# Forgetting attention: value products of an even and an odd head as one piece of TensorE's work, alternating block by block

## The chip, the cores and the metric

The kernel runs on one core of a Trainium2 chip. The metric is the device time of one execution in microseconds. Before the change three runs took 1273.55, 1274.48 and 1274.74 us; the median is 1274.48 us.

## What is computed

Two decoder layers on 512 tokens, with 16 learned meta tokens ahead of them (528 rows, 1024 features, fp32). Each layer projects its rows into the inputs of three mixers (retention, pooling, forgetting attention), puts their outputs side by side, projects them back, adds the residual and normalises; then a gated feed-forward layer does the same. The change is in the forgetting attention, which has six heads of 64 features:

```python
c = jnp.cumsum(logf.astype(jnp.float32), axis=1).transpose(0, 2, 1)
qf = q.astype(jnp.float32) * (d ** -0.5)
...
s = jnp.einsum('bihd,bjhd->bhij', qb, kf)
s = s + cb[..., :, None] - c[..., None, :]
mask = (kpos[None, :] <= qpos[:, None]) & key_ok[None, :]
s = jnp.where(mask, s, NEG_INF)
p = jax.nn.softmax(s, axis=-1)
return jnp.einsum('bhij,bjhd->bihd', p, vf)
```

The last line is the one whose order of work changes.

## The kernel before

**Staging.** The tokens are cut into five chunks: 16 meta tokens (chunk 0), then four of 128 (chunks 1 to 4). Large products (input weights, output weights, feed-forward) run with every operand split in a high and a low part, three products each: lines 195, 196 and 197 (`mm3`). Weights come from memory as chunks of 128 x 1024, are split by ScalarE (line 174) and by VectorE or GpSimd (line 138), and are kept in four buffers.

**What sets the order.** TensorE's program order is made by `Plan`: each run of its work is a `Piece` with an assumed cost, dependencies with assumed delays (the table `LAG`), a priority, and a count of the buffers that it holds. `Plan.run` walks a clock of assumed times and takes, of the pieces that should be ready and whose buffers fit, the first by priority. Pieces of attention have priority 5, the products of the input weights 9, so the latter fill the time between. The times are assumptions that decide the order alone; on the chip TensorE executes that order and waits where an input isn't there. The other engines' instructions are put in order by the framework.

**Forgetting attention**, per chunk c = 1 to 4 and head h = 0 to 5, over the key blocks of 128 tokens up to the chunk's own (c blocks):
- `fox_q` (lines 621 to 630) splits two heads' queries; GpSimd makes the low part (`qb`).
- `fox_score` (667 to 684): two products for the scores (lines 634 and 635; for chunk 4 four, into the one buffer `s2`), then masked with a maximum on VectorE (679), Exp with a sum on ScalarE (680), and scaled by the reciprocal of the sum on VectorE (682) and, for the meta tokens, on GpSimd (683).
- `fox_turn` (686 to 693): one transpose per block on TensorE (691) into PSUM, and a copy into a buffer `pt` (693), by VectorE for even heads and by ScalarE for odd ones.
- `fox_value` (695 to 703): one product per block, accumulated in PSUM tile `o`. The output has 64 partitions: the lower 64 for even heads, the upper 64 for odd ones; heads 0 and 1 share columns 0 to 127, 2 and 3 the next 128, 4 and 5 the next.
- `fox_meta` (705 to 716): the transposed weights of the meta tokens (708), and their products onto `o` (714), after which the chunk goes to the mix.

A value product is plain fp32 and leaves two records in the trace. Its stationary operand has 128 rows and 64 columns. Scores and `pt` share seven buffers `tmp` by tag, and `holds` counts them; `one` are four PSUM buffers. Pooling's sums (`pool_sums`, lines 816 to 834) run on VectorE in the same stage, and `pool_mix` (841) at its end. After it come the output weights' products over `mixAf` and `mixBf`.

## Time and profile before

| | us |
|---|---|
| median of three runs | 1274.48 |
| span of the profiled execution | 1271.5 |
| TensorE busy | 1234.6 |
| VectorE busy | 646.6 |
| ScalarE busy | 479.9 |
| GpSimd busy | 337.7 |
| value products (line 701), 240 records, busy | 30.3 |
| transposes (line 691), 120 records, busy | 21.1 |

The page gives the profiled execution's span, from its first to its last instruction; its time from outside is not given apart from the three runs, whose median is 3.0 us above that span. Records of TensorE overlap: a product's record lasts from its start to its modelled end, while the next starts already. How long a run of products holds up the engine is read from the starts in the timeline of the trace: from one group's start to the next group's start. A row of the timeline has start, duration, engine, line, operation, tiles, stationary shape, moving shape and the count of records put together (x8).

### The profile page before, as it was taken

The numbers are of one execution on the slowest core, as the hardware profiler recorded it, in microseconds if no ns is written. First come the engines' busy times: TensorE is split into PE (matmuls) and PEld (weight loads), VectorE is DVE, ScalarE is ACT, GpSimd is POOL, SyncE is SP. The second block draws the span as 40 slices with busy tenths as digits, with TensorE's granted clock in tenths as the row PEclk, the third lists the DMA queues.
The fourth block names the chain that finished last, engine by engine and source line by source line (L and its number), as shares of the span: only waits on it lengthen the run. The fifth ranks groups of instructions, "written<-read, shape, count | busy, mean of one in ns | idle before, by whom it ended". The sixth has DMA issues, their size and how long they took to land. (4 is left out here: it accounts for less than half of the span.)

```text
span 1271.5 us, 21413 instructions
## 1 busy us (share of the span) xinstructions
PE 1234.6 (97%) x8650; PEld 1145.8 (90%) x8650; DVE 646.6 (51%) x1257; ACT 479.9 (38%) x893; POOL 337.7 (27%) x375
## 2 busy tenths in 40 slices
PE   7999999889999999999999999998999999999997
PEld 6999989889999999999999899997888888888886
DVE  7575677963333333333384756789632333332226
ACT  5436544543232232222264366455423232221112
POOL 5423339740001100010055243498600000000004
PEclk9999999999999999999999999999899999999999
DMA  6431212423222223233343221134222232222222
GB/s 231 125 99 51 68 34 101 135 98 100 96 88 86 98 84 96 77 90 92 108 143 123 80 80 59 34 118 153 94 84 99 85 99 95 88 100 100 99 91 75
DMA packets 41506, 122.58 MB, mean 96 GB/s; under 512 B 6392, under 2 KB 12696, under 8 KB 41408
## 3 DMA queue, kind: packets, MB, share of 16 engines
q1 hardware_dynamic: 41408, 121.22, 29.1%
q8 instruction: 68, 1.11, 0.4%
q14 instruction: 30, 0.25, 0.1%
HBM read 115.22 MB, written 2.10 MB: 92 GB/s over the span
## 5 line engine op out<-in xcount | busy, mean ns | idle before, releaser
L195 PE MATMUL acc<-xh,w 128*128 128x256 f32 (+2 forms) x1920 | 589.7, 307 | 0.4 <-DVE ka L138 0.4
L196 PE MATMUL acc<-xl,w 128*128 128x256 f32 (+2 forms) x1920 | 582.0, 303 | 1.5 <-POOL xl L138 1.0
L197 PE MATMUL acc<-xh,w 128*128 128x256 f32 (+2 forms) x1920 | 581.8, 303 | 0.0
L138 DVE TENSOR_TENSOR w<-raw,w 128x1024 fp32r<-128x1024 f32 (+1 forms) x181 | 217.4, 1203 | 332.7 <-ACT w L174 332.4
L195 PEld LDWEIGHTS acc<-xh,w 128*128 128x128 f32 x1920 | 363.4, 189 | 18.1 <-issue 1.6
L196 PEld LDWEIGHTS acc<-xl,w 128*128 128x128 f32 x1920 | 364.1, 190 | 16.4 <-POOL xl L138 1.9
L197 PEld LDWEIGHTS acc<-xh,w 128*128 128x128 f32 x1920 | 363.1, 189 | 13.7
L174 ACT CAST w<-raw 128x1024 fp32r<-128x1024 f32 (+1 forms) x211 | 218.8, 1038 | 301.7 <-PE acc L197 121.1
L138 POOL TENSOR_TENSOR w<-raw,w 128x256 fp32r<-128x256 f32 (+1 forms) x74 | 120.6, 1635 | 69.7 <-ACT w L174 61.7
L361 POOL TENSOR_TENSOR y<-xh,xl 128x256 f32<-128x256 f32 (+1 forms) x64 | 51.2, 827 | 225.2 <-DVE g8Bl L138 93.8
L256 POOL TENSOR_TENSOR r<-r,mhalf 128x1 f32<-128x1 f32 (+3 forms) x18 | 14.7, 819 | 324.6 <-DVE r L255 324.6
L138 POOL TENSOR_TENSOR xl<-y,xh 128x256 fp32r<-128x256 f32 (+1 forms) x57 | 49.6, 886 | 22.3 <-ACT xh L271 16.3
L981 ACT ACTIVATE y<-acc 128x272 f32<-128x272 f32 (+1 forms) x44 | 17.2, 392 | 89.0 <-PE acc L197 89.0
L981 ACT ACTIVATE sa<-acc 128x512 f32<-128x512 f32 (+1 forms) x24 | 13.5, 563 | 88.4 <-PE acc L197 88.4
L984 DVE TENSOR_TENSOR sa<-sa,acc 128x512 f32<-128x512 f32 (+1 forms) x24 | 15.4, 642 | 59.0 <-PE acc L197 57.9
L285 DVE SCALAR_TENSOR_TENSOR y<-y,acc 128x256 f32<-128x256 f32 (+1 forms) x48 | 20.1, 420 | 44.5 <-PE acc L197 44.3
L984 DVE TENSOR_TENSOR y<-y,acc 128x272 f32<-128x272 f32 (+1 forms) x44 | 18.9, 429 | 40.4 <-PE acc L197 40.4
L290 POOL TENSOR_TENSOR y<-y 128x256 f32<-128x256 f32 (+1 forms) x12 | 11.0, 914 | 106.3 <-DVE y L285 106.3
L294 ACT ACTIVATE y<-y 128x256 f32<-128x256 f32 (+1 forms) x42 | 17.6, 419 | 54.6 <-DVE y L285 54.5
L680 ACT ACTIVATE p<-p,sm 128x144 f32<-128x144 f32 (+3 forms) x48 | 27.6, 574 | 17.7 <-DVE sm L679 16.1
L683 POOL TENSOR_SCALAR pm<-p,sm 128x16 f32<-128x16 f32 x48 | 21.8, 455 | 43.8 <-DVE sm L681 42.5
L290 DVE TENSOR_TENSOR y<-y 128x256 f32<-128x256 f32 (+1 forms) x30 | 32.1, 1071 | 2.5 <-POOL y L290 1.2
(1000 smaller groups left out, 1916.9 us busy)
## 6 DMA issues: line engine op xcount, KB each, us to landing
raw<-in_w SPq DMA_DIRECT2D x88, 512.0 KB, 3.3
raw<-in_w_in SPq DMA_DIRECT2D x42, 512.0 KB, 4.0
raw<-in_w_out SPq DMA_DIRECT2D x32, 512.0 KB, 3.4
raw<-in_w2b SPq DMA_DIRECT2D x22, 512.0 KB, 3.3
raw<-in_w2a SPq DMA_DIRECT2D x18, 512.0 KB, 3.4
raw<-in_w2a SPq DMA_DIRECT2D x9, 384.0 KB, 3.2
xin<-in_x SPq DMA_DIRECT2D x4, 512.0 KB
out<-y SPq DMA_DIRECT2D x12, 128.0 KB, 1.8
```

Of the source, the lines that this page charges most:

```text
L138: return eng.tensor_tensor(lo, full, hi.bitcast(F32), op=ALU.subtract)
L174: nc.scalar.copy(w[:, 0, :n], raw[:, :n])
L195: nc.tensor.matmul(ps, lhsT=wh, rhs=hi, start=first, stop=False)
L196: nc.tensor.matmul(ps, lhsT=wh, rhs=lo, start=False, stop=False)
L197: nc.tensor.matmul(ps, lhsT=wl, rhs=hi, start=False, stop=last)
L285: nc.vector.scalar_tensor_tensor(y, y, ALPHA, ps, op0=ALU.mult, op1=ALU.add)
L290: (nc.gpsimd if CFG[f"s{i}"] else nc.vector).tensor_tensor(self.s, self.seen[0] if i == 1 else self.s, y, op=ALU.add)
L361: nc.gpsimd.tensor_tensor(y, hi[:, o:].bitcast(F32), lo[:, o:].bitcast(F32), op=ALU.add)
L680: nc.scalar.activation(out=p[:, :NM + nk], in_=p[:, :ce], func=AF.Exp, scale=-1.0, bias=sm[:, 0:1], accum_out=sm[:, 1:2])
L683: nc.gpsimd.tensor_scalar(F[c, "pm"][:, h, :], p[:, :NM], sm[:, 2:3], 1.0, op0=ALU.mult, op1=ALU.mult)
L981: nc.scalar.activation(out=s, in_=ps, func=AF.Silu)
L984: nc.vector.tensor_tensor(s, s, ps, op=ALU.mult)
```

## The change

The values of heads 2i and 2i + 1 become one piece. Its loop goes over the key blocks, and in each block does the even head's product and then the odd head's. The piece waits for both heads' transposes and holds both `pt` buffers. Its assumed cost is 0.26 us per block for two heads, where it was 0.16 per block and head. Products, operands and sums are the same, and so are all other pieces. Below line 712 the lines of the changed kernel move down by 3, in the plan by 3 to 7: 701 becomes 704, 708 becomes 711, 714 becomes 717, 841 becomes 844. The other lines of the diff drop comments and docstrings.

```diff
-        def fox_value(c, h):
+        def fox_value(c, i):
+
             nk = CH[c][1] - NM
-            if h == 0:
+            if i == 0:
                 F[c, "o"] = one()
-            o, pt = F[c, "o"], F.pop((c, "pt", h))
+            o, pts = F[c, "o"], [F.pop((c, "pt", 2 * i + j)) for j in range(2)]
             for b in range(nk // P):
-                nc.tensor.matmul(o[64 * (h % 2):64 * (h % 2) + 64, (h // 2) * P:(h // 2 + 1) * P],
-                                 lhsT=vt["vf"][:, b, h * 64:(h + 1) * 64], rhs=pt[:, b * P:(b + 1) * P],
-                                 start=(h < 2 and b == 0), stop=False, skip_group_check=True)
+                for j, pt in enumerate(pts):
+                    h = 2 * i + j
+                    nc.tensor.matmul(o[64 * j:64 * j + 64, i * P:(i + 1) * P],
+                                     lhsT=vt["vf"][:, b, h * 64:(h + 1) * 64], rhs=pt[:, b * P:(b + 1) * P],
+                                     start=(i == 0 and b == 0), stop=False, skip_group_check=True)
...
                 tn = add(lambda c=c, h=h: fox_turn(c, h), 0.11 * (nk // P), [(sc_, lag("p") + nk / 450.0)], 5)
-                prev_v = add(lambda c=c, h=h: fox_value(c, h), 0.16 * (nk // P),
-                             [(tn, lag("pt")), prev_v] + [(vf[b], lag("vt")) for b in range(1, c + 1)], 5)
                 sc_.holds("tmp", 2, tn)
+                if h % 2 == 0:
+                    even = tn
+                    continue
+                prev_v = add(lambda c=c, h=h: fox_value(c, h // 2), 0.26 * (nk // P),
+                             [(even, lag("pt")), (tn, lag("pt")), prev_v] + [(vf[b], lag("vt")) for b in range(1, c + 1)], 5)
+                even.holds("tmp", 1, prev_v)
                 tn.holds("tmp", 1, prev_v)
-                if h == 0:
+                if h == 1:
                     first_v = prev_v
```

Since costs and dependencies of the pieces change, the plan puts other work differently too. Three places on TensorE show it.

In layer 0, chunk 3, the order before has these rows, the values of two heads (L701) with the scores of a later head between them:

```order
L197 MATMUL acc<-xh,w 128x256
L701 MATMUL one<-pt,vtf 64x128 x3
L634 MATMUL one<-ka,qa 128x400
L635 MATMUL one<-kb_1115,qb_136 128x400
L701 MATMUL one<-pt,vtf 64x128 x3
L691 MATMUL one<-c_ident,p 128x128 x3
```

In the changed kernel the same chunk has:

```order
L197 MATMUL acc<-xh,w 128x272
L704 MATMUL one<-pt,vtf 64x128 x6
L691 MATMUL one<-c_ident,p 128x128 x3
L634 MATMUL one<-ka,qa 128x400
L635 MATMUL one<-kb_1115,qb_136 128x400
```

Two runs of three products have become one of six. Over the whole kernel the order has 33 runs of value products before and 20 now.

At the start of chunk 4 in layer 0 stand, before, the values and transposes of a head of chunk 3 and then the first scores of chunk 4 (tile `s`):

```order
L701 MATMUL one<-pt,vtf 64x128 x3
L691 MATMUL one<-c_ident,p 128x128 x3
L634 MATMUL s_2299<-ka,qa 128x272
L635 MATMUL s_2299<-kb_133,qb_137 128x272
L634 MATMUL s_2299<-ka,qa 128x256
L635 MATMUL s_2299<-kb_133,qb_137 128x256
L195 MATMUL acc<-xh,w 128x272
```

and now a pair of chunk 3, the first scores of chunk 4, and the transposes of the last two heads of chunk 3 with those of the meta tokens (L711):

```order
L704 MATMUL one<-pt,vtf 64x128 x6
L634 MATMUL s_2301<-ka,qa 128x272
L635 MATMUL s_2301<-kb_133,qb_137 128x272
L634 MATMUL s_2301<-ka,qa 128x256
L635 MATMUL s_2301<-kb_133,qb_137 128x256
L691 MATMUL one<-c_ident,p 128x128 x6
L711 MATMUL one<-c_ident,pm 96x128
```

The scores of chunk 4 have moved ahead of two heads' transposes.

At the end of layer 1's mixing the order before has the last products of the input weights, pooling (L841) and the first output weights; values and meta products (L701, L714) stand 39 and 24 products earlier:

```order
L195 MATMUL acc<-xh,w 128x256
L196 MATMUL acc<-xl,w 128x256
L197 MATMUL acc<-xh,w 128x256
L841 MATMUL one<-pu_7523,pw 128x256
L841 MATMUL one<-pu_7524,pw 128x256
L841 MATMUL one<-pu_7523,pw 128x256
L841 MATMUL one<-pu_7524,pw 128x256
L195 MATMUL acc<-mixAf,w 128x256
```

The changed kernel has there:

```order
L197 MATMUL acc<-xh,w 128x256
L844 MATMUL one<-pu_7523,pw 128x256
L844 MATMUL one<-pu_7524,pw 128x256
L704 MATMUL one<-pt,vtf 64x128 x8
L844 MATMUL one<-pu_7523,pw 128x256
L844 MATMUL one<-pu_7524,pw 128x256
L717 MATMUL one<-pmt,vbd 128x128 x3
L195 MATMUL acc<-mixAf,w 128x256
```

The last pair and the meta products now come after the last input weights.

## The prediction

> **What bounds the kernel now.** I read the page first, then the busy time by stage, the waits of TensorE in the two stages that the change touches, and last the order of time around single runs of value products, where the prices are.

> ```profile
> span 1271.5 us, 21413 instructions
> PE 1234.6 (97%) x8650; PEld 1145.8 (90%) x8650; DVE 646.6 (51%) x1257; ACT 479.9 (38%) x893; POOL 337.7 (27%) x375
> ...
> core 0: us, PE busy (x) PEld busy (x) DVE busy (x) ACT busy (x) POOL busy (x), PEclk, DMA share, GB/s
> 130.00:160.00 30.00, 29.39 (x242) 27.25 (x242) 20.97 (x63) 16.61 (x45) 11.98 (x18) 1.00 0.17 55
> 160.00:200.00 40.00, 39.47 (x305) 35.27 (x304) 30.06 (x68) 17.48 (x40) 21.11 (x26) 1.00 0.13 41
> 770.00:800.00 30.00, 30.00 (x238) 26.84 (x236) 23.24 (x69) 19.17 (x51) 11.73 (x20) 1.00 0.11 37
> 800.00:835.00 35.00, 35.00 (x280) 32.64 (x280) 23.32 (x50) 14.45 (x32) 22.04 (x26) 1.00 0.14 46
> ```

> TensorE (PE) is busy 1234.6 of 1271.5 us. The forgetting attention of layer 0 lies at about 115 to 200 us and that of layer 1 at about 740 to 830. In the four windows PE is busy 133.9 of 135 us, at a granted clock of 1.00; the next engine, VectorE (DVE), is busy 97.6. In these stages PE has hardly a hole, so time taken from its row comes off the end, unless a hole opens. The holes that are there:

> ```profile
> PE one L708 <- ACT pt L693: 0.6, 1, 0.6
> PE one L691 <- DVE p L682: 0.5, 1, 0.5
> ...
> PE acc L196 <- DVE xl L845: 0.4, 1, 0.4
> ```

> Two waits of 1.1 us together in layer 0 (135 to 201 us), one of 0.4 us in layer 1 (768 to 843 us).

> **The value products as they are.** A busy PE is not a PE at its peak, so I read starts, not durations. One fp32 product leaves two records.

> ```profile
> L701 PE MATMUL one<-pt,vtf x240: 272/273/324, 139.7 to 827.0; 128*64 128x128 f32 x120
> ...
> 181.69 0.29 PE L196 MATMUL acc<-xl,w 128*128 128x272 f32 x1
> 181.82 0.28 PE L197 MATMUL acc<-xh,w 128*128 128x272 f32 x1
> 182.04 1.09 PE L701 MATMUL one<-pt,vtf 128*64 128x128 f32 x8
> 183.06 0.44 PE L691 MATMUL one<-c_ident,p 128*128 128x128 f32 x2
> ...
> 160.03 0.28 PE L197 MATMUL acc<-xh,w 128*128 128x256 f32 x1
> 160.24 0.87 PE L701 MATMUL one<-pt,vtf 128*64 128x128 f32 x6
> 161.04 0.44 PE L691 MATMUL one<-c_ident,p 128*128 128x128 f32 x2
> ...
> 150.18 0.38 PE L691 MATMUL one<-c_ident,p 128*128 128x128 f32 x2
> 150.49 0.65 PE L701 MATMUL one<-pt,vtf 128*64 128x128 f32 x4
> 151.07 0.39 PE L195 MATMUL acc<-xh,w 128*128 128x272 f32 x1
> ```

> These are runs of one head over four, three and two key blocks (8, 6, 4 records). From the first record to the next other product they take 183.06 - 182.04 = 1.02, 0.80 and 0.58 us: 0.22 us for each further block, thus 0.11 us a record. The step into a run is 0.21 or 0.22 us, where a product otherwise follows after 0.12 or 0.13 (181.69 to 181.82). So a run adds to PE's row: four blocks 0.22 + 1.02 - 0.13 = 1.11 us, three 0.21 + 0.80 - 0.12 = 0.89, two 0.20 + 0.58 - 0.11 = 0.67 (the step from the second transpose is 150.49 - 150.18 less the 0.11 between the two).

> Now the runs in which heads of both parities already stand side by side:

> ```profile
> 139.66 0.88 PE L701 MATMUL one<-pt,vtf 128*64 128x128 f32 x12
> 140.46 0.39 PE L634 MATMUL one<-ka,qa 128*128 128x272 f32 x1
> ...
> 147.81 0.67 PE L701 MATMUL one<-pt,vtf 128*64 128x128 f32 x8
> 148.40 0.44 PE L691 MATMUL one<-c_ident,p 128*128 128x128 f32 x2
> ...
> 779.16 1.09 PE L701 MATMUL one<-pt,vtf 128*64 128x128 f32 x12
> 780.18 0.44 PE L691 MATMUL one<-c_ident,p 128*128 128x128 f32 x2
> ...
> 800.15 1.15 PE L701 MATMUL one<-pt,vtf 128*64 128x128 f32 x12
> 801.23 0.39 PE L634 MATMUL s<-ka,qa 128*128 128x272 f32 x1
> ```

> At 139.66 the six heads of the first chunk, one block each, alternate even and odd: twelve records in 0.80 us, exactly what six records of one head took. At 147.81 two heads of two blocks each take 0.59 us, where one head alone took 0.58. So an even and an odd head, whose outputs lie in the lower and the upper 64 partitions, run beside each other, and **a pair costs what one head costs**. The run at 800.15 sets the limit: two heads of three blocks, all blocks of one and then all of the other, take 1.08 us, not 0.80; without alternation only part overlaps.

> [...]

> **Term 1, the runs.** In the timeline of the trace layer 0 has 17 runs: one of the first chunk, for two blocks 8, 4, 4 and 8 records, then six of 6 and six of 8. Layer 1 has 16: one of the first chunk, 12 (779.16), 4, 4, 4, then four of 6 and one of 12 (800.15), then six of 8. Afterwards the order has ten in each layer: the first chunk's, unchanged, and three pairs for each other chunk, all alternating.
> - Layer 0: two blocks go from 4 x 0.67 to 3 x 0.67, saving 0.67; three blocks from 6 to 3 x 0.89, saving 2.67; four blocks from 6 to 3 x 1.11, saving 3.33. Sum 6.67 us.
> - Layer 1: two blocks from (0.20 + 1.02 - 0.11 = 1.11) + 3 x 0.67 to 3 x 0.67, saving 1.11; three blocks from 4 x 0.89 + (0.21 + 1.08 - 0.12 = 1.17) to 3 x 0.89, saving 2.06; four blocks 3.33. Sum 6.50 us.

> Together **-13.2 us**. A pair of four blocks stands nowhere in the trace; I price it as one head, as for the three shapes seen. If it behaved like the run at 800.15, a pair of three or four blocks would cost 0.28 us more, 12 pairs 3.4 us. The whole cost of the other case stands under the rivals.

> **Term 2, new waits.** Every transpose follows its scores by a chain: mask and maximum on DVE (L679), Exp on ACT, scaling on DVE (L682). Until now one run of values per head stood somewhere between; now one per two heads. The cover of a chain shrinks by about half a run, 0.45 to 0.55 us. First and last of the tight ones:

> ```profile
> 168.63 0.28 PE L635 MATMUL s<-kb,qb 66*128 66x256 f32 x1
> ...
> 175.97 0.60 PE L691 MATMUL one<-c_ident,p 128*128 128x128 f32 x4
> ...
> 165.00 2.12 DVE L682 TENSOR_SCALAR p<-p,sm 128x384 f32<-128x384 f32 x1
> 167.04 1.24 DVE L820 TENSOR_TENSOR pb<-pu 128x543 f32<-128x543 f32 x1
> ...
> 172.07 0.69 DVE L679 CUSTOM_DVE_ANT_0 p<-s,mask 128x528 f32<-128x528 f32 x1
> ...
> 175.26 0.53 DVE L682 TENSOR_SCALAR p<-p,sm 128x512 f32<-128x512 f32 x1
> ...
> 810.23 0.48 DVE L682 TENSOR_SCALAR p<-p,sm 128x512 f32<-128x512 f32 x1
> ...
> 811.08 0.60 PE L691 MATMUL one<-c_ident,p 128*128 128x128 f32 x4
> ```

> Chunk 4, head 0 of layer 0: scores at 168.63, scaled at 175.79, transposed from 175.97: 0.18 us to spare, since pooling sums (L820 and on) kept DVE until 172.07. Chunk 4, head 2 of layer 1: scaled at 810.71, transposed from 811.08, 0.37 us to spare. Of the 24 heads of chunks 3 and 4 in both layers, six have less than 0.6 us. Each can lose at most the run that leaves, 1.11 us: bound 6 x 1.11 = 6.7 us; the other end is nothing, since the order also moves other work (the pooling sums now come after chunk 4's first mask). I take 6 x (0.55 - 0.3 to spare) = 1.5, plus 0.5 for the displaced sums: **+2.0 us**. Queued behind a waiting transpose is all of PE.

> The pair also waits for the odd head's copy. That costs nothing while the twelve weight products between copy and values remain, and the order keeps them in both layers for the last chunk, except at the end of layer 1, where six and two pooling products stand instead. If that cover went, the copy would show:

> ```profile
> 179.75 0.74 ACT L680 ACTIVATE p<-p,sm 128x528 f32<-128x528 f32 x1
> ...
> 180.48 0.58 ACT L693 COPY pt<-one 128x512 f32<-128x512 f32 x1
> ```

> The copy ends at 181.06, 0.98 us ahead of its values (182.04). That the even head's buffer is held longer, and that DVE and GpSimd get new orders, I put at nothing: the scores of the next pair stand ahead of the values in the order, so the seven buffers last. If they did not, see the slower rival.

> **Term 3, the end of layer 1.** Pooling products, a pair and the meta product now follow the last input weights, where pooling products alone stood. The wait of 0.4 us on L845 has some 2 us more cover: **-0.4 us**, between -0.6 and 0, or +0.5 if the four PSUM buffers are short there.

> After both stages PE runs on output weights, with DVE and POOL behind it:

> ```profile
> 200.00:230.00 30.00, 30.00 (x232) 29.32 (x230) 24.44 (x31) 15.71 (x27) 24.60 (x18) 1.00 0.35 123
> ```

> PE has no hole there and all arrives earlier by the same amount, so I count the gain as passed on.

> **Sum.** -13.2 + 2.0 - 0.4 = -11.6 us. The page gives the profiled execution's span, 1271.5 us; the three runs have a median of 1274.48, 3.0 us for what lies around it. The span falls to 1259.9, the time to **1262.9 us**.

> **Rivals.**
> - *Waits eat half.* All six tight chains lose a whole run: -13.2 + 6.7 = -6.5, 1268.0 us. For it: spare times of 0.18 and 0.37. Against: waits of only 1.1 and 0.4 us today. Chance 0.18 (1265.5 to 1269).
> - *No more overlap than now*: accumulating over four blocks keeps the two heads apart, and the change does not do what it says. Pairs over two, three and four blocks then cost what runs of four, six and eight blocks cost, 1.11, 1.55 and 1.99 (0.22 a block), three of each 13.95 a layer, against 14.68 and 14.51 now. Saved 1.3, less the 2.0 of waits: 1275.2 us, no change that can be told. Against it the row at 147.81. Chance 0.08. [...]
> - *Slower: a shortage of buffers.* The pair holds both heads' transposed weights until the odd one comes; if then the next scores cannot be written, score, transpose and values come one after the other on PE. A chain's own work is 0.69 + 0.74 + 0.53 = 1.96 us (L679, L680, L682 in the rows above). It decides at 13.2 / 18 pairs = 0.73 us each; with half of the chain to be seen, 1 us each, the time is 1274.5 - 13.2 + 18 = 1279.3. Against: the order has scores ahead of values. Chance 0.04.

> **How the numbers follow.** Forecast 0.70 (1260.3 to 1265.5), waits 0.18, no overlap 0.08, slower 0.04. The low end is -13.2 - 0.6 with no new wait, and some rounding; the high end 1269 takes in the waits. What lies outside is about 0.14. A difference under 0.2% (2.5 us) can't be told from none: faster 0.88, same 0.08, slower 0.04.

> **What would show it.** Right: 20 runs of values in place of 33, those of two heads over four blocks with 16 records and 1.02 us to the next product, three blocks 0.80, two 0.59; PE's wait for L682 and L693 up to about 3 us. Wrong: 16 records in 1.9 us (no overlap), or PE waits for p and pt above 6 us, or a new hole in the windows that follow.

## The result, and the profile after

The changed kernel takes 1284.87 us (median of four runs, 1282.71 to 1287.4), the kernel before 1274.01 beside it: ratio 1.0091, 95% interval 1.0079 to 1.0103. The change costs 10.9 us where a gain of 11.6 was forecast. The profiled execution's own time was 1285.74 us, 1.7 us above its span. Its page, and its busy time by stage (the columns are those shown of before):

```profile
span 1284.0 us, 21407 instructions
PE 1232.6 (96%) x8650; PEld 1144.9 (89%) x8650; DVE 650.2 (51%) x1257; ACT 480.1 (37%) x893; POOL 340.1 (26%) x375
...
160.00:200.00 40.00, 32.40 (x267) 30.32 (x266) 30.77 (x73) 17.09 (x40) 15.60 (x19) 0.91 0.12 39
200.00:230.00 30.00, 29.44 (x235) 28.44 (x233) 22.73 (x28) 15.47 (x28) 29.02 (x26) 1.00 0.30 102
...
800.00:835.00 35.00, 31.10 (x254) 28.64 (x254) 28.13 (x57) 13.32 (x30) 11.32 (x12) 0.90 0.09 31
```

Two things are new in the attention's windows. TensorE is busy 32.40 of 40 us where it had 39.47, and 31.10 of 35 where it had 35.00; and its granted clock, 1.00 before, is 0.91 and 0.90. GpSimd's work has moved: 15.60 us in 160 to 200 (21.11 before), 29.02 in 200 to 230 (24.60 before). The waits of TensorE name the holes (total, times, longest):

```profile
PE one L691 <- DVE p L682: 11.0, 3, 4.1
...
PE one L844 <- DVE xl L848: 1.1, 1, 1.1
```

Three waits of transposes for scaled scores make 11.0 us, where one of 0.5 us stood. The pairs themselves cost what was forecast. In the timeline of TensorE, with the next group behind each run:

```profile
148.36 0.66 PE L704 MATMUL one<-pt,vtf 128*64 128x128 f32 x8
148.95 0.44 PE L691 MATMUL one<-c_ident,p 128*128 128x128 f32 x2
...
166.76 1.55 PE L704 MATMUL one<-pt,vtf 128*64 128x128 f32 x12
168.24 0.57 PE L691 MATMUL one<-c_ident,p 128*128 128x128 f32 x3
...
804.00 0.88 PE L704 MATMUL one<-pt,vtf 128*64 128x128 f32 x12
804.80 0.38 PE L195 MATMUL acc<-xh,w 128*128 128x256 f32 x1
...
201.58 1.09 PE L704 MATMUL one<-pt,vtf 128*64 128x128 f32 x16
202.60 0.39 PE L195 MATMUL acc<-xh,w 128*128 128x256 f32 x1
...
823.35 0.43 PE L704 MATMUL one<-pt,vtf 128*64 128x128 f32 x2
824.20 1.09 PE L704 MATMUL one<-pt,vtf 128*64 128x128 f32 x14 [0.42 <-ACT pt L693]
```

8, 12 and 16 records take 0.59, 0.80 and 1.02 us, within 0.01, in 15 of the 20 runs. One more (172.04) takes 0.85. Two runs of 12 records, at 166.76 and 814.52, take 1.48 us: they point at the clock. Two others, both in layer 1, wait inside the run for the odd head's copy, which ScalarE does behind an Exp (from 823.58 and 799.52): the one at 823.35 takes 1.88 us instead of 1.02, one of 12 records at 799.46 takes 1.38 instead of 0.80. That is 1.4 us. The rows around the first long wait for p, 3.54 us (in brackets: the idle time and what ended it):

```profile
159.62 0.49 PE L691 MATMUL one<-c_ident,p 128*128 128x128 f32 x3
163.64 0.52 PE L691 MATMUL one<-c_ident,p 128*128 128x128 f32 x3 [3.54 <-DVE p L682]
...
164.62 0.29 PE L197 MATMUL acc<-xh,w 128*128 128x272 f32 x1
164.74 0.29 PE L195 MATMUL acc<-xh,w 128*128 128x272 f32 x1
...
165.95 0.43 PE L195 MATMUL acc<-xh,w 128*128 128x272 f32 x1
166.18 0.43 PE L196 MATMUL acc<-xl,w 128*128 128x272 f32 x1
```

About 1.3 us after TensorE resumes, the step from product to product goes from 0.12 to 0.23 us. Short windows behind the three waits give the granted clock:

```profile
165.00:173.00 8.00, 8.00 (x62) 7.11 (x60) 4.99 (x18) 3.97 (x12) 3.33 (x6) 0.79 0.12 45
...
185.00:187.00 2.00, 0.99 (x5) 1.02 (x6) 1.51 (x4) 0.83 (x2) 0.57 (x1) 0.60 0.00 0
187.00:194.00 7.00, 7.00 (x60) 6.70 (x60) 3.67 (x11) 2.64 (x6) 0.58 (x2) 0.87 0.01 2
...
811.00:816.00 5.00, 5.00 (x29) 4.43 (x29) 4.73 (x12) 1.59 (x4) 0.79 (x1) 0.50 0.01 2
816.00:822.00 6.00, 6.00 (x50) 6.00 (x49) 4.34 (x10) 2.38 (x7) 1.29 (x2) 0.93 0.01 3
```

Length times what is missing of the clock is 1.7 + 0.8 + 0.9 + 2.5 + 0.4, about 6 us on top of the 11.0. Each of the three waits, of 3.54, 4.06 and 3.41 us, has the half clock at its end or behind it; the trace also has it behind two shorter waits, shown below.

Why were the scaled scores late? VectorE's queue at the three places:

```profile
159.58 0.17 DVE L834 TENSOR_TENSOR pt<-pc,c_icnt 64x16 f32<-64x16 f32 x1
159.68 0.69 DVE L836 SCALAR_TENSOR_TENSOR pu<-pc,pu 64x512 f32<-64x512 f32 x1
160.40 0.17 DVE L835 TENSOR_TENSOR pu<-pt,pu 64x16 f32<-64x16 f32 x1
...
160.98 2.51 DVE L682 TENSOR_SCALAR p<-p,sm 128x384 f32<-128x384 f32 x1
...
180.27 1.92 DVE L834 TENSOR_TENSOR pt<-pc,c_icnt 64x16 f32<-64x16 f32 x1
...
183.52 0.14 DVE L681 RECIPROCAL sm<-sm 128x1 f32<-128x1 f32 x1
...
185.38 0.48 DVE L682 TENSOR_SCALAR p<-p,sm 128x512 f32<-128x512 f32 x1
...
806.06 2.85 DVE L836 SCALAR_TENSOR_TENSOR pu<-pb,pu 64x512 f32<-64x512 f32 x1
808.84 0.15 DVE L681 RECIPROCAL sm<-sm 128x1 f32<-128x1 f32 x1
809.02 0.69 DVE L836 SCALAR_TENSOR_TENSOR pu<-pc,pu 64x512 f32<-64x512 f32 x1
809.74 0.72 DVE L823 TENSOR_TENSOR pb<-pu 128x543 f32<-128x543 f32 x1
810.38 0.41 DVE L682 TENSOR_SCALAR p<-p,sm 128x384 f32<-128x384 f32 x1
```

and GpSimd at the same times, splitting a chunk of output weights:

```profile
160.94 2.34 POOL L138 TENSOR_TENSOR w<-raw,w 128x1024 fp32r<-128x1024 f32 x1 [0.51 <-ACT w L174]
...
179.53 2.62 POOL L138 TENSOR_TENSOR w<-raw,w 128x1024 fp32r<-128x1024 f32 x1 [0.99 <-ACT w L174]
...
805.78 2.59 POOL L138 TENSOR_TENSOR w<-raw,w 128x1024 fp32r<-128x1024 f32 x1 [0.39 <-ACT w L174]
```

Each late scaling (L682) or its reciprocal (L681) stands behind sums of the pooling (L823 to L836), and one operation of VectorE in each place lasts until GpSimd's split is done, or a little longer: in the first place the scaling itself (2.51 us), in the second L834 (0.17 us at 159.58, 1.92 at 180.27), in the third L836 (0.69 and 2.85). For the two later ones ScalarE had done its part long before:

```profile
179.99 0.19 ACT L680 ACTIVATION_READ_ACCUMULATOR p<-p,sm 128x1 f32 x1
...
804.58 0.19 ACT L680 ACTIVATION_READ_ACCUMULATOR p<-p,sm 128x1 f32 x1
```

From its end, 180.18 and 804.77, to the start of the scaling, 185.38 and 810.38, the scores lay 5.2 and 5.6 us on VectorE's queue. Before, the same had happened under cover (the L682 of 2.12 us at 165.00, beside a split of 2.38 us at 164.52).

By stage, from the starts in the two traces:

| start of | before | after | difference |
|---|---|---|---|
| first value product, layer 0 | 139.66 | 140.21 | +0.55 |
| first product over `mixAf`, layer 0 | 203.14 | 206.38 | +3.24 |
| last product over `mixBf`, layer 0 | 253.96 | 260.11 | +6.15 |
| first value product, layer 1 | 770.31 | 777.80 | +7.49 |
| first product over `mixAf`, layer 1 | 833.76 | 844.74 | +10.98 |
| last product over `mixBf`, layer 1 | 883.55 | 897.06 | +13.51 |
| end of the span | 1271.52 | 1283.96 | +12.44 |

The attention stages lose 2.7 and 3.5 us, although their products became cheaper. The terms add up: -13.2 for the pairs, +11.0 for the waits for p, about +6 for the clock behind them, +1.4 for the copies and +1.1 for the wait of L844 make 6.3 us (smaller waits left out), and the table has 6.2.

The output weights behind them lose another 2.9 and 2.5, and the trace shows where. In both layers TensorE waits there for a `y` of the norm (L312 on L298), 1.97 and 2.07 us, where it waited 1.71 and 1.82 before. Behind these two waits the granted clock is now 0.50 for 3.4 us (236.60 to 240.00 and 874.90 to 878.30), where before it was 1.00; the step between products shows it:

```profile
236.51 0.86 PE L312 MATMUL one<-c_ident,y 128*128 128x128 f32 x3 [1.97 <-DVE y L298]
...
237.59 0.41 PE L197 MATMUL acc<-xh,w 128*128 128x256 f32 x1
237.81 0.41 PE L195 MATMUL acc<-xh,w 128*128 128x256 f32 x1
```

That is 1.7 us in each layer; the waits of these stages together are 0.6 and 0.8 us longer than before. GpSimd now does work there that has moved out of the attention (29.02 of 30 us, above); whether this makes `y` late was not tried by itself.

### The profile page after: what moved, and what is told of

It reads as the page before. It is cut to its first block, busy times and chain, and to the rows that moved or that the text cites. A ratio compares the mean times of both kernels' runs of the same rounds, so it can differ in the third digit from the quotient of the medians.

```text
span 1284.0 us, 21407 instructions
## 1 busy us (share of the span) xinstructions
PE 1232.6 (96%) x8650; PEld 1144.9 (89%) x8650; DVE 650.2 (51%) x1257; ACT 480.1 (37%) x893; POOL 340.1 (26%) x375
## 3 DMA queue, kind: packets, MB, share of 16 engines
q8 instruction: 68, 1.11, 0.3%
## 5 line engine op out<-in xcount | busy, mean ns | idle before, releaser
L195 PE MATMUL acc<-xh,w 128*128 128x256 f32 (+2 forms) x1920 | 591.7, 308 | 0.4 <-DVE ka L138 0.4
L196 PE MATMUL acc<-xl,w 128*128 128x256 f32 (+2 forms) x1920 | 584.6, 304 | 2.1 <-POOL xl L138 1.9
L197 PE MATMUL acc<-xh,w 128*128 128x256 f32 (+2 forms) x1920 | 584.1, 304 | 0.0
L196 PEld LDWEIGHTS acc<-xl,w 128*128 128x128 f32 x1920 | 366.0, 191 | 17.7 <-POOL xl L138 3.4
L195 PEld LDWEIGHTS acc<-xh,w 128*128 128x128 f32 x1920 | 365.4, 190 | 17.6 <-issue 1.1
L197 PEld LDWEIGHTS acc<-xh,w 128*128 128x128 f32 x1920 | 365.4, 190 | 13.6
L285 DVE SCALAR_TENSOR_TENSOR y<-y,acc 128x256 f32<-128x256 f32 (+1 forms) x48 | 20.1, 419 | 49.5 <-PE acc L197 49.5
L680 ACT ACTIVATE p<-p,sm 128x144 f32<-128x144 f32 (+3 forms) x48 | 27.5, 574 | 22.0 <-DVE sm L679 21.5
```

The costliest lines, as they stand in the source:

```text
L195: nc.tensor.matmul(ps, lhsT=wh, rhs=hi, start=first, stop=False)
L196: nc.tensor.matmul(ps, lhsT=wh, rhs=lo, start=False, stop=False)
L197: nc.tensor.matmul(ps, lhsT=wl, rhs=hi, start=False, stop=last)
L285: nc.vector.scalar_tensor_tensor(y, y, ALPHA, ps, op0=ALU.mult, op1=ALU.add)
L680: nc.scalar.activation(out=p[:, :NM + nk], in_=p[:, :ce], func=AF.Exp, scale=-1.0, bias=sm[:, 0:1], accum_out=sm[:, 1:2])
```

## The experiments

Each kernel was timed against the kernel before on the same chip (medians 1272.3 to 1273.3; four groups on different chips, so a difference of 1 or 2 us between kernels of different groups says little). Theory **order**: the pairs are cheaper as priced, and the plan's new order costs more than they save. Rival **pair**: something in the paired products themselves costs it. Rival **power**: overlapping products draw the clock down.

**Pairs, with the old order.** The plan is that of before; the even head's piece issues nothing, the odd head's issues both. Against the changed kernel:

```diff
+            if h % 2 == 0:
+                return
+            i = h // 2
...
-                if h % 2 == 0:
-                    even = tn
-                    continue
-                prev_v = add(lambda c=c, h=h: fox_value(c, h // 2), 0.26 * (nk // P),
-                             [(even, lag("pt")), (tn, lag("pt")), prev_v] + [(vf[b], lag("vt")) for b in range(1, c + 1)], 5)
+                prev_v = add(lambda c=c, h=h: fox_value(c, h), 0.16 * (nk // P),
+                             [(tn, lag("pt")), prev_v] + [(vf[b], lag("vt")) for b in range(1, c + 1)], 5)
-                even.holds("tmp", 1, prev_v)
                 tn.holds("tmp", 1, prev_v)
```

> The plan of before, piece by piece and cost by cost; only the even head's values are held back and done with the odd head's, alternating. TensorE's other products, and all of GpSimd's work, keep the order of before. Theory order (pairs are as cheap as the runs show; the loss came from the order that the plan made around them: scaled p behind pooling sums and behind a GpSimd weight split, then a halved clock): 13.2 us under before less up to 2 of waits, 1261 to 1264 us, no wait for L682 above 1 us, granted clock 1.00 from 160 to 200 us. Theory pair (waiting for two heads and holding two buffers is what costs): 1280 or more. Theory power (overlapping products draw the clock down): 1267 to 1270, clock about 0.9 in the same stretch.

1269.0 us, ratio 0.9969 (0.9957 to 0.998): faster than before, so theory pair falls, and the new order costs 16 us. The time lies in the range that power gave, not in that of order; but only some 4 of the 13.2 us arrive, and for power the clock would have to be down. The waits, and the window of layer 0:

```profile
PE one L691 <- DVE p L682: 4.6, 5, 1.2
...
160.00:200.00 40.00, 36.42 (x323) 33.72 (x323) 31.05 (x70) 18.04 (x42) 22.88 (x29) 1.00 0.11 41
```

The waits for p are there, but short (at most 1.2 us), and the clock stays at 1.00, so power falls too.

**The new order, heads one after the other.** In the changed kernel the two loops change places, so all blocks of the even head come first.

```diff
-            for b in range(nk // P):
-                for j, pt in enumerate(pts):
+            for j, pt in enumerate(pts):
+                for b in range(nk // P):
```

> The changed kernel, but within the piece all blocks of the even head and then all of the odd one. Same plan, same order of everything else. Theory order: pairs of three and four blocks cost 0.28 us more each, 12 of them, so up to 3.4 us slower than the changed kernel (1285 to 1288), runs of 16 records about 1.3 us to the next product. If alternation inside the piece does nothing beyond being adjacent: the same time as the changed kernel and 1.02 us.

1284.55 us, 1.0095 (1.0072 to 1.0118): as slow as the change. Its runs of value products are dearer:

```profile
172.44 1.14 PE L704 MATMUL one<-pt,vtf 128*64 128x128 f32 x12
173.51 0.39 PE L634 MATMUL s<-ka,qa 128*128 128x272 f32 x1
...
199.12 1.58 PE L704 MATMUL one<-pt,vtf 128*64 128x128 f32 x16
200.63 0.66 PE L691 MATMUL one<-c_ident,p 128*128 128x128 f32 x4
```

1.07 and 1.51 us in place of 0.80 and 1.02. With six pairs of each that is 6 x 0.27 + 6 x 0.49 = 4.6 us more work on TensorE, an estimate from these runs. No cost shows at the end, but the two intervals together leave some 3 us open either way, so it stays open how much of it is hidden. The waits for p are again 11.0 us in three.

**First splits on VectorE.** The low parts of the first two output-weight chunks of half A (the tokens up to chunk 2) are made by VectorE.

```diff
-        wout_u.append({h: [add_chunks(d["w_out"][l, m], 1024, nc.gpsimd if CFG[f"o{m}"] else nc.vector)
+        wout_u.append({h: [add_chunks(d["w_out"][l, m], 1024, nc.gpsimd if CFG[f"o{m}"] and not (h == "A" and m < 2) else nc.vector)
```

> The changed kernel with the low parts of the first two output-weight chunks of half A, in both layers, made by VectorE and no longer by GpSimd. Theory order: the VectorE operations of 2.51, 1.92 and 2.85 us that end with a GpSimd split go back to 0.4 to 0.7, the three long waits of TensorE shrink from 3.5, 4.1 and 3.4 to about 1.5 to 2 each, and shorter holes leave the clock at 1.00: 1272 to 1278 us. Theories pair and power: 1283 to 1287, no change.

1277.22 us, 1.0049 (1.0029 to 1.0069). The ratios put what goes with the splits alone at 5 us, the medians at 7 to 8; the five runs scatter, three from 1276.3 to 1277.2 and two above 1281. The profile is of a run of 1281.18 us: its waits for p fall to 4.2 us, while waits for L681 come to 4.0 (the longest 3.5) and for `y` of L285, in the output stages, to 5.4, and the clock is 0.96 and 0.95 in the two windows. So the time came as order said, but the long waits did not all go.

**Sums after the scores.** Both sums of the pooling depend on the last head's transposes.

```diff
-        us_ = {m: add(lambda m=m: pool_sums(m), 0.0, both(("u", m)), 5) for m in range(2)}
+        us_ = {m: add(lambda m=m: pool_sums(m), 0.0, both(("u", m)) + [tn], 5) for m in range(2)}
```

> The changed kernel with both pooling sums put after the last head's transposes. Theory order: no pooling sum stands in front of a scaled p, so the three long waits fall under 1 us each and the clock stays at 1.00; against that, pooling's products come later behind the first output weights, 1 to 4 us. 1266 to 1271 us. Theories pair and power: 1283 or more.

1288.0 us, 1.0119 (1.0103 to 1.0136): wrong in the time, which by itself fits the rivals. But the waits for p fell to 0.4 us and the clock is 1.00 in 160 to 200 and 800 to 835; the sums came too late for their own products:

```profile
PE one L844 <- DVE pu L835: 7.5, 1, 7.5
PE one L844 <- DVE pu L836: 7.3, 1, 7.3
```

One wait took the other's place.

**The change without the sums.** `pool_sums` issues nothing; TensorE's order is that of the change.

```diff
         def pool_sums(m):
-            L = NM + T
...
+            pass
```

> The change as it is, with the sums of the pooling left out (their result is not computed), TensorE's order the same. Theory order (the pooling's sums stand ahead of p on VectorE's queue, and GpSimd's splits stretch them): the three long waits for p of 11.0 us vanish, the clock stays at 1.00 in both stages, 1260 to 1264 us. Theory splits alone (the stretched operations cost it, whatever stands there): 1275 to 1279. Theory pair (the pair's products themselves cost it): 1280 or more.

1272.45 us, 0.9995 (0.9986 to 1.0004). The waits for p fall from 11.0 to 0.4 us, the clock is 1.00 in both stages, and the first product over `mixAf` in layer 0 starts at 197.07, 6.07 us ahead of before. That is nearly the whole of Term 1 (6.67 for this layer): the sums on VectorE's queue cause the long waits. The time was still missed by 8 us. At the last product over `mixBf` the lead in layer 0 is down to 3.33 us, so output weights took back almost half. In layer 1 the leads are 6.54 and 4.58; but 3.55 us of lead stood at the start of that stage already, so it passed on 3.0 of its 6.50 us, and what held the rest was not tried. The last feed-forward stage then lost 2.9 us more (its products follow after 230 to 240 ns, before after 227); why stays open.

**What in the change makes the order.** First the assumed cost of a pair:

```diff
-                prev_v = add(lambda c=c, h=h: fox_value(c, h // 2), 0.26 * (nk // P),
+                prev_v = add(lambda c=c, h=h: fox_value(c, h // 2), 0.32 * (nk // P),
```

> The change with 0.32 in place of 0.26 us a block in the plan, which is what two heads cost the plan before; all else as the change has it. Theory number (the lower cost lets the plan start later pieces sooner and so set the pooling's sums and GpSimd's splits against the late heads): back towards the pairs in the old order, 1267 to 1272 us, TensorE's waits for p below 5 us. Theory waiting (what reorders the plan is that a pair becomes ready only with its odd head, whatever it costs): 1281 to 1288, the long waits still there.

and, as another edit of the same line:

```diff
-                prev_v = add(lambda c=c, h=h: fox_value(c, h // 2), 0.26 * (nk // P),
+                prev_v = add(lambda c=c, h=h: fox_value(c, h // 2), 0.23 + 0.22 * (nk // P),
```

> The change with the measured cost of a pair in the plan (0.23 + 0.22 us a block, so 0.67, 0.89 and 1.11) in place of 0.52, 0.78 and 1.04. Theory number: a truer cost gives a better order, 1270 to 1278 us. Theory waiting: no better, 1281 to 1288. In either case a long wait for p is to go with a sum of the pooling or a stretched operation ahead of it on VectorE's queue.

1281.3 us (1.0066; 1.0049 to 1.0082) and 1284.64 (1.0091; 1.0076 to 1.0106): the number is not the cause. The first is 3.6 us below the change; both lie in the range of theory waiting. Then the pairs in the old order, with one thing put back, the hold of the even head's buffer until the pair is done:

```diff
-                tn.holds("tmp", 1, prev_v)
+                if h % 2:
+                    even.holds("tmp", 1, prev_v)
+                    tn.holds("tmp", 1, prev_v)
+                else:
+                    even = tn
```

> Paired products, but the plan sees two pieces as before (0.16 us a block and head, the even head's issuing nothing, the odd head's both), and the buffers of both weights' transposes held until the pair is done. Only the holds differ from the pairs in the old order (1269.0 us). Theory waiting: the plan's order stays near the old one, 1267 to 1273. Rival (holding the even head's buffer longer is what reorders it): 1280 to 1288.

1282.56 us (1.0073; 1.0056 to 1.0089), 13.6 above the same kernel without it. The theory that a pair's waiting for its odd head reorders the plan falls; the rival, the hold, stands. So the same lines went alone into the kernel before, which has no pairs:

> The kernel before, single-head value products and all costs, with one line changed: the plan counts an even head's buffer of transposed weights as taken until the odd head's value products. Theory hold (this count alone reorders the plan and sets the pooling's sums and GpSimd's splits against the late heads): 1279 to 1287 us, as slow as the pairs with the same holds (1282.56), with waits for p above 6 us. Rival (the hold costs only where pairs make TensorE's stretches shorter): 1271 to 1276.

1289.47 us (1.0128; 1.0111 to 1.0145), 16 us slower than before, and even slower than expected. On VectorE the sums have moved. Two rows of this kernel (its line 820 opens a sum of the pooling):

```profile
166.86 0.42 DVE L682 TENSOR_SCALAR p<-p,sm 128x384 f32<-128x384 f32 x1
...
171.11 0.72 DVE L820 TENSOR_TENSOR pb<-pu 128x543 f32<-128x543 f32 x1
```

Before, the first sum starts at 150.16, after 10 of the layer's 24 scalings; here at 171.11, after the 18 of chunks 1 to 3, and the second follows 2.5 us later with no scaling between, ahead of all heads of the last chunk. The longest wait for p, 3.62 us, ends at 178.53, behind a scaling at 177.91 whose Exp was done at 172.23. From 166 to 179 no operation of VectorE lasts longer than 0.72 us, so here its queue made the wait without one stretched to 2 us. Two more kernels give the plan's count, and that alone, one more buffer, while the pool keeps its seven:

```diff
-    plan = Plan({"acc": 2, "s2": 1, "one": 3, "tmp": 7, "y": 23, "Q": 2})
+    plan = Plan({"acc": 2, "s2": 1, "one": 3, "tmp": 8, "y": 23, "Q": 2})
```

> The change as it is, with eight buffers of this tag in the plan's count, while the pool has seven as before. Theory hold (the plan, short of a buffer in its count, sorts the scores and sums later): with one more in the count the sums come earlier again, 1267 to 1276 us, waits for p below 6 us. Rival (the real seven buffers then run short, or a pair's readiness is what delays): 1280 to 1288.

> The pairs planned by heads (1282.56 us) with eight buffers in the plan's count, the pool with seven. Theory hold: 1265 to 1273 us, near the pairs in the old order (1269.0). Rival: 1278 to 1286.

1275.58 us (1.0017; 1.0008 to 1.0027) for the change, 1273.37 (1.0005; 0.9996 to 1.0014) for the pairs planned by heads: 9 us back in both, and the real seven buffers suffice. The first time lies in its range (its waits for p, 6.4 us, a little above), the second 0.4 us above. All of them beside each other, with the count of the layer's 24 scalings that start ahead of the first and of the second sum in the trace:

| kernel | us | waits for p, us | ahead of the sums, layer 0 | layer 1 |
|---|---|---|---|---|
| before | 1274.01 | 0.5 | 10 and 17 | 16 and 19 |
| pairs, old order | 1269.0 | 4.6 | 10 and 17 | 16 and 19 |
| by heads, count of 8 | 1273.37 | 7.0 | 17 and 19 | 13 and 20 |
| change, count of 8 | 1275.58 | 6.4 | 17 and 18 | 12 and 18 |
| cost of before | 1281.3 | 9.9 | 18 and 18 | 15 and 18 |
| by heads | 1282.56 | 11.4 | 18 and 18 | 18 and 18 |
| measured cost | 1284.64 | 10.9 | 18 and 18 | 12 and 18 |
| change | 1284.87 | 11.0 | 12 and 18 | 16 and 17 |
| hold alone | 1289.47 | 7.3 | 18 and 18 | 18 and 18 |

The counts don't put the kernels in the order of their times. With a count of 8 the sums did not come earlier again in layer 0, as expected (17 scalings ahead of the first, 12 in the change), and in layer 1 of the change the first sum stands where it stood before. So it is shown that the hold in the plan's count costs the time, and that in the change the sums ahead of p make the long waits; by which steps of the plan the one leads to the other is not. The waits for p are not the whole loss: hold alone has fewer of them than the change, and is slower. How the rest of it splits was not followed further.

**Why only 4 of 13.2 us arrive in the old order.** VectorE's queue was the suspect, so the copies of the transposes (line 693) went to ScalarE for all heads, in the pairs and in the kernel before:

```diff
-            (nc.scalar.copy if h % 2 else nc.vector.tensor_copy)(pt[:, :nk], tp[:, :nk])
+            nc.scalar.copy(pt[:, :nk], tp[:, :nk])
```

> Pairs in the old order (1269.0 us) with all copies of the weights' transposes on ScalarE. Theory queue (what the pairs uncover is VectorE's queue, which runs just behind TensorE in this stage: its copies are about 5.8 us a layer, 3 x (0.28 + 0.41 + 0.55 + 0.68)): TensorE waits less for VectorE's p, 1263 to 1267 us. Rival (the remaining waits are only for stretched operations beside GpSimd's splits, not for the load of the queue): 1268 to 1270.

> The kernel before with the same copies on ScalarE, as the control: with single-head value products TensorE is long enough to cover VectorE's queue, so no change, 1272 to 1275 us by theory queue. If it gains as much as the pairs in the old order do, the copies are a gain of their own and say nothing on the pairs.

Pairs: 1268.82 us (0.9964; 0.9951 to 0.9977), as without it, and where the rival had it. Control: 1273.37 (1.0004; 0.9994 to 1.0013), no change. In the profiled runs the first product over `mixAf` in layer 1 starts 7.5 us ahead of before, where it was 4.7 without the copies, yet the span gains only 0.9. So in these single traces the load of the queue bounds the stage in part, but most of what it frees is lost behind it.

The trace of the pairs in the old order says where the 13.2 us stay. From the first value product to the first product over `mixAf` the two layers gain 2.8 and 3.8 us. The other 6.6 are nearly all new idle time of TensorE in these two stages: the waits for p (4.6 us), one of 0.9 for an Exp (L680), one of 0.3 for a mask (L679), and pairs that wait for a copy. Last, with the first splits on VectorE as well:

> Pairs in the old order, copies on ScalarE, and the low parts of the first two output-weight chunks on VectorE in place of GpSimd. Theory splits (VectorE's operations are held up beside GpSimd's splits): 1 to 3 us below the pairs in the old order with copies on ScalarE. Rival (VectorE's queue is the bound): the two low parts add about 2 us to that queue, same or 1 to 2 us above it.

1266.39 us (0.9945; 0.993 to 0.996), the fastest of all, 2.4 below the one before, as theory splits had it. Three waits for p remain, none above 1.3 us:

```profile
PE one L691 <- DVE p L682: 3.6, 3, 1.3
```

## Why the prediction was wrong

- **Term 1 (-13.2 us)** was right in mechanism and price: 0.59, 0.80 and 1.02 us, four blocks included, which no row of before had shown. The rival "no more overlap" fell. (The run of 16 records in 1.88 us looks like its sign, but waits for a copy.)
- **The step that failed** stands under Term 2: "That the even head's buffer is held longer, and that DVE and GpSimd get new orders, I put at nothing: the scores of the next pair stand ahead of the values in the order, so the seven buffers last." The seven on the chip do last: with a count of 8 in the plan they served for 1275.58 us. But the plan counts them, and with the longer hold it makes another order: the hold alone costs 16 us, and one more buffer in the count gives 9 us of the change back. In the new order sums of the pooling stand ahead of p on VectorE, which is the other half of what was put at nothing: without them the 11.0 us of waits fall to 0.4.
- **Term 2's size.** +2.0, bound 6.7, came from taking runs away from the cover of six chains, with the chains' own times as before. The waits were 11.0 us, and none of the three fell on one of the six: they met head 1 of chunk 3 and head 1 of chunk 4 in layer 0 and head 5 of chunk 3 in layer 1, which before had 2.25, 2.65 and 0.68 us to spare. Their chains themselves grew: 5.2 and 5.6 us from Exp to scaling for the two later ones. The half clock behind them, about 6 us, had no term at all, nor had that behind the waits for `y` in the output stages, 3.4 us. The prediction had quoted the L682 of 2.12 us and the sums that "kept DVE until 172.07", but not asked what they cost in another place.
- **The odd head's copy** "costs nothing while the twelve weight products between copy and values remain". Twelve stood there, and two pairs of layer 1 still waited, 1.4 us together.
- **"Time taken from its row comes off the end, unless a hole opens"**: with the old order 4 us of 13.2 arrived. The pairs uncovered waits that TensorE's longer work had hidden. "I count the gain as passed on" through the output weights failed too: without the sums a lead of 6.1 us was 3.3 behind them.
- **Term 3 (-0.4 us)**: the wait of 0.4 us for the low part did go. But the last pooling product now waits 1.1 us for L848, which reads a result of pooling out of PSUM; the product doesn't use what L848 writes, so it waits for the buffer. That is the prediction's own "+0.5 if the four PSUM buffers are short there". It is the same without the sums.
- **The slower rival** had the right place, the longer hold of the buffers, and the wrong mechanism: it let engines wait for a buffer and set 0.73 us a pair as the point that decides. The 11.0 us are waits for a value, not for a buffer. Its 1279.3 us is 5.6 below the time.
- Of the signs named, two came: waits for p above 6 us, and longer waits in the windows that follow.
- A small thing in the working: the listed chances leave 0.12 outside the range, not 0.14.

## What to carry to other kernels

Where a planner sets the order, an edit to what a piece holds is an edit to the order of every engine: run the new order with the old products, and the new products in the old order, before pricing either. Look at what an off-path engine does next to the path's chain (here sums and splits that were harmless under cover), and price it where the new order puts it. Look at the granted clock behind a long idle stretch of TensorE: here stretches of 1.97 and 2.07 us cost more than their length, with a clock of 0.50 for 3.4 us behind each.
